# Dense matmuls inside the block inverses, a reordered load in the third quarter, and eight temporaries in a hybrid RWKV-7 and sparse-attention layer

## The chip, the cores and the metric

The kernel runs on one core of one Trainium2 chip. The metric is the device time of one execution in microseconds (us). Times of the kernel before are a median of three runs. A separate execution is recorded by the hardware profiler; its own time is given beside them. Engines are named as in the profile: PE is TensorE, DVE is VectorE, ACT is ScalarE, POOL is GpSimd, SP is the engine that only issues DMAs. A small q after an engine's name stands for its instruction sequencer, where DMA issues are shown.

## The reference

One decoder layer over 1024 tokens of width 1024, in float32. A normalised input is multiplied by one wide matrix. Its columns feed two branches that are computed side by side and merged by sigmoid gates:

```python
proj = rmsnorm(h, norm1_g) @ w_in            # -> p_rwkv, p_att, p_idx, p_gate
y_a = rwkv7_mix(token_shift(p_rwkv, tshift_mu), ...)
y_b = dsa_attention(rope(q), rope(k), v, rope(q_idx), rope(k_idx), w_idx)
g_a, g_b = split(sigmoid(p_gate))
h = h + (g_a * (y_a @ w_o_rwkv) + g_b * (y_b @ w_o_att)) @ w_out
h = h + (silu(z_gate) * z_up) @ w_ffn_out    # z = rmsnorm(h) @ w_ffn_in
return rmsnorm(h, normf_g)
```

The RWKV branch is a recurrence over tokens with a 64 x 64 state for each of 8 heads:

```python
sa = einsum('bhij,bhj->bhi', state, -kk_t)
state = state * d_t + sa[..., None] * (kk_t * a_t) + v_t[..., None] * k_t
y_t = einsum('bhij,bhj->bhi', state, r_t)
```

The attention branch lets each query see the 256 keys with the highest index scores.

## The kernel before, in words

**Two kinds of matmul.** The wide products (projections, gates, output matrices, feed-forward) are split into high and low parts so that three matmuls of 128 x 128 by 128 x 512 make one product of near-float32 accuracy. `mm3` (lines 137 to 149) issues them and is a generator: it yields after every few matmuls how many it has issued. This text calls them dense matmuls. The RWKV branch works on small tiles with long chains between PE, ACT and DVE.

**Filling.** Generators of dense work wait in a queue named `fill`. `pump(n)` (lines 177 to 186) adds n to a credit and runs the first generator until the credit is used up; a generator that yields more than is left makes the credit negative, which the next call pays off. So dense matmuls stand between the small ones, at places and in numbers that are written into the code. `ticks(n, m)` (lines 190 to 194) pumps n in m portions and after each portion advances a second generator, `beside[0]`, by one step: a bisection for the attention's selection (`select`, lines 979 to 1054), which runs on ACT and DVE. The order of instructions on PE is the order of the program text (manual_schedule, line 1700). The order on ACT, DVE, POOL and SP is fixed when the program is built, by a list scheduler that follows program order as far as it believes operands and buffers to be ready. At run time each engine and each DMA queue works through its list in order.

**Temporaries.** `tmp()` (lines 112 and 113) gives a 128 x 512 float32 tile from the pool `tp`, which has 4 such slots (line 58). A slot is free again when the last reader of the tile is done, and that can be a DMA that stores it. Tiles from `tmp()` hold gate values on their way to DRAM (lines 515 to 518), parts of the selection (lines 1029 to 1032), the attention's result on its way to DRAM (lines 1171, 1190 and 1191) and the gates that the merge loads (lines 1281 to 1284).

**The RWKV quarters.** `rwkv` (lines 548 to 909) handles 512 tokens per call, in two quarters of 256. Quarter q has two pairs of 64-token chunks, `pr` 0 and 1. In each quarter:

- Lines 701 to 722: masked products `MT` are made, and their 32 x 32 diagonal blocks are stored to DRAM (`d_n`, line 721).
- Lines 740 to 753: the blocks are loaded with other axes (`N`, line 742) and DVE inverts them by a recursion of 31 steps in `W`.
- Lines 754 to 767: the inverses go through DRAM (`d_w`, lines 755 and 764) into `TT`; DVE transposes a part of them into `TZ` (line 767).
- Lines 769 to 774: a row of sums is loaded, broadcast over 64 partitions (`P`, line 771), and POOL multiplies it (line 774).
- Line 775: `ticks` covers this chain with dense matmuls.
- Lines 778 to 785: for each `pr`, 32 x 32 matmuls (line 781) from `TZ` into PSUM, and ACT copies them back to `TZ` (line 784).
- Lines 787 to 798: `inner(0)`, a product for the right-hand side (line 791), then `pump(4)`.
- Lines 799 to 806: for each `pr`, the second 32 x 32 matmuls (line 802), which read that copy; ACT copies the result to `TT` (line 805).
- Lines 832 to 909: the recurrence over four chunks with three matmul groups each (lines 843, 862 and 874), with pumps between.

While quarters 0 and 1 run, `fill` holds projections, gates and the attention of the first 512 tokens (`att0`). From quarter 2 on it holds `merge(0)` and the feed-forward part of the first 512 tokens (`ffn`). `merge` (lines 1274 to 1340) loads two gate tiles per output column block d in `gates(d)` (lines 1280 to 1284), those of d = 0 ahead of the rest. All of the loads and stores named here are issued by SP, except the gate stores of line 518, which ACT issues, as it does the weight loads of line 123 in this part of the kernel.

Of the kernel before, what the change touches and what calls it, by code (L numbers as in the profile page):

```python
# [51 lines left out]
def block_kernel(ctx: ExitStack, tc: tile.TileContext, ins: dict, outT: bass.AP, outR: bass.AP, stop=None, dbg=None):  # L52
    nc = tc.nc
    V, A, G, T, SY = nc.vector, nc.scalar, nc.gpsimd, nc.tensor, nc.sync

    cp = ctx.enter_context(tc.tile_pool(name="cp", bufs=1))
    wp = ctx.enter_context(tc.tile_pool(name="wp", bufs=2))
    tp = ctx.enter_context(tc.tile_pool(name="tp", bufs=4))
    dp = ctx.enter_context(tc.tile_pool(name="dp", bufs=1, space=bass.MemoryType.DRAM))
    psA = ctx.enter_context(tc.tile_pool(name="psA", bufs=3, space=bass.MemoryType.PSUM))  # L60
    psM = ctx.enter_context(tc.tile_pool(name="psM", bufs=5, space=bass.MemoryType.PSUM))
# [24 lines left out]
    def scratch(name, shape):  # L86
        return [dp.tile(shape, F32, name=f"{name}{h}") for h in range(2)]
# [8 lines left out]
    d_g = scratch("d_g", [16, 128, HT])  # L96
# [4 lines left out]
    d_bs = [dp.tile([2, 4, 256], F32, name=f"d_bs{q}") for q in range(4)]  # L101
    d_n = [dp.tile([64, 32, 32], F32, name=f"d_n{q}") for q in range(4)]
# [74 lines left out]
    def pump(n):  # L177

        credit[0] += n
        while credit[0] > 0 and fill:  # L180
            try:
                credit[0] -= abs(next(fill[0]))
            except StopIteration:
                fill.popleft()
        if not fill:
            credit[0] = 0
# [3 lines left out]
    def ticks(n, m):  # L190

        for i in range(m):
            pump(n * (i + 1) // m - n * i // m)
            next(beside[0], None)
# [331 lines left out]
    def rwkv_consts(p):  # L526
# [18 lines left out]
        p.tile([128, 64], F32, name="edge")  # L545
        return cmask, wup, gup, rmask, ind, ind16

    def rwkv(half, p, consts, ready=None, settled=None):
        cmask, wup, gup, rmask, ind, ind16 = consts

        def t4(tag, shape=(128, 4, 256)):
            return p.tile(list(shape), F32, tag=tag, name=tag)

        for q in range(2 * half, 2 * half + 2):
# [184 lines left out]

            N = p.tile([128, 32, 32], F32, tag="x6", name="N")  # L740
            for par_ in range(2):
                SY.dma_start(N[64 * par_:64 * par_ + 64], d_n[q])
            W = p.tile([128, 16, 32], F32, tag="x7", name="W")
            V.memset(W, 0.0)
            for par_ in range(2):
# [22 lines left out]

            bsp = t4("P")
            for e in range(2):  # L770
                SY.dma_start(bsp[64 * e:64 * e + 64].rearrange("p c t -> p (c t)"),
                             d_bs[q][e].rearrange("c s -> (c s)").partition_broadcast(64))
            bon = v
            G.tensor_tensor(bon, v, bsp, op=ALU.mult)
            ticks((209, 231, 281, 232)[q], (13, 4, 10, 6)[q])
            both = [(h, pa, 64 - 64 * pa, 64 * pa) for h in range(8) for pa in range(2)]
            hd = [(h, h // 2, slice((h % 2) * 64, (h % 2) * 64 + 64), slice(h * 64, h * 64 + 64)) for h in range(8)]
            for pr in range(2):
                ps = mix()
                for h, pa, ba, kb in both:  # L780
                    T.matmul(ps[ba + 32:ba + 64, h * 32:(h + 1) * 32], MT[2 * pr + pa][ba:ba + 32, h, ba + 32:ba + 64],
                             TZ[ba:ba + 32, 0, pr, h, :], start=True, stop=True)
                for ba in (64, 0):
                    A.activation(TZ[ba + 32:ba + 64, 1, pr, :, :],
                                 ps[ba + 32:ba + 64, 0:256].rearrange("p (h t) -> p h t", h=8), AF.Copy)

            def inner(pr):
                ps = mix()
# [44 lines left out]
            for pr in range(2):  # L833
                yb = p.tile([128, 2, 512], F32, tag=("P", "x6")[pr], name="yb")
                yc, y2 = yb[:, 0, :], yb[:, 1, :]
                for pa in range(2):
                    c = 2 * pr + pa
# [436 lines left out]
    def merge(half, zp, zs):  # L1274
        yt = yhi, ylo = act_tiles(zp, "y", ("s0", "s1"))
        mt = act_tiles(zp, "m", ("s2", "s3"))
        for j in range(8):
            SY.dma_start(ylo[:, j, :].bitcast(F32), (d_ya if j < 4 else d_yb)[half][j % 4])

        def gates(d):  # L1280
            ga, gb = tmp(), tmp()
            SY.dma_start(ga, d_g[half][d])
            SY.dma_start(gb, d_g[half][8 + d])
            return ga, gb

        first_gates = gates(0) if half == 0 else None
        yield 0
        for j in range(8):
            split(yhi[:, j, :], ylo[:, j, :], ylo[:, j, :].bitcast(F32))
        yield -30  # L1290
        ahead = [weights(ins["w_o"][d]) for d in range(2)] if half == 0 else []
        for d in range(8):
            w = ahead[d] if d < len(ahead) else weights(ins["w_o"][d])
            ga, gb = first_gates if half == d == 0 else gates(d)
            pa = acc()
            pb = None
            if half == d == 0:
                pb = acc()
                yield from mm3_two((pa, pb), w, yt)
            else:  # L1300
                yield from mm3(pa, w, yt, nk=4)
            with tc.high_priority() if pb else nullcontext():
                V.scalar_tensor_tensor(ga, ga, 1.0, pa, op0=ALU.add, op1=ALU.mult)
                if pb:
                    V.scalar_tensor_tensor(gb, gb, 1.0, pb, op0=ALU.add, op1=ALU.mult)
            if pb is None:
                pb = acc()
                yield from mm3(pb, w, yt, nk=4, wk=4, ak=4)
                V.scalar_tensor_tensor(gb, gb, 1.0, pb, op0=ALU.add, op1=ALU.mult)
            V.tensor_tensor(ga, ga, gb, op=ALU.add)  # L1310
            A.activation(mt[0][:, d, :], ga, AF.Copy, scale=0.5)
            V.scalar_tensor_tensor(mt[1][:, d, :], ga, 0.5, mt[0][:, d, :].bitcast(F32), op0=ALU.mult,
                                   op1=ALU.subtract)
        yield -10
        h = zp.tile([128, 8, HT], F32, tag="s0", name="h")
        load_x(half, h, range(8))
        sq = Rms(h)
        zt = zhi, zlo = act_tiles(zp, "z", ("s1", "s3")) if half == 0 else (None, None)
        pss = []
        if half == 0:  # L1320
            pss = [acc(), acc()]
            yield from mm3_last(pss, [weights(ins["w_out"][d]) for d in range(2)], mt, 8)
        for d in range(8):
            if d < len(pss):
                ps = pss[d]
            else:
                ps = acc()
                yield from mm3(ps, weights(ins["w_out"][d]), mt)
            V.tensor_tensor(h[:, d, :], h[:, d, :], ps, op=ALU.add)
            if half == 0:  # L1330
                A.activation(zhi[:, d, :], h[:, d, :], AF.Copy, scale=par[:, P_N2 + d:P_N2 + d + 1])
            SY.dma_start(d_h[half][d], h[:, d, :])
            sq.add(d)
        if half == 1:
            zs.append(sq)
            return
        for d in range(8):
            V.scalar_tensor_tensor(zlo[:, d, :], h[:, d, :], par[:, P_N2 + d:P_N2 + d + 1],
                                   zhi[:, d, :].bitcast(F32), op0=ALU.mult, op1=ALU.subtract)
        zs.extend((zt, sq))  # L1340
# [548 lines left out]
```

## Time and profile before

| what | value |
|---|---|
| median of 3 runs | 1706.21 us (1706.05 to 1706.52) |
| profiled execution, its own time | 1709.14 us |
| its span, first to last instruction | 1707.2 us |
| mean granted clock of TensorE | 0.996 |
| first 32 x 32 matmuls (line 781) of quarters 0, 1, 2, 3 | 426.5, 575.5, 739.4, 895.0 us |
| busy time of PE, DVE, ACT, POOL | 1686.1, 1180.9, 896.4, 97.3 us |

How to read it: the page has six sections: busy time by engine, a picture of the span in 40 slices, DMA queues, the chain of work that ended last, the costliest groups of instructions, and DMA issues. Other views of the same trace list who waited for whom, the instructions in order of time, and the busy time in chosen stretches. In the view in order of time each row has the start, the length, the engine, the line, the operation, the tiles (written <- read), the shapes, how many were merged, and in brackets the idle time before it with what ended it. Matmuls overlap: a matmul's own length is longer than the distance to the next one's start.

### The profile page before, as it was taken

The page shows a single profiled execution, that of the slowest core. Times are in us where ns is not written, and L with a number is a line of the kernel's source. Part 1 is how long each engine was busy: PE and PEld are TensorE (multiplying, and loading weights), DVE is VectorE, ACT ScalarE, POOL GpSimd, SP SyncE. Part 2 cuts the span into 40 slices and gives each one's busy share as a digit, 9 for nine tenths or more (in the row PEclk, how much of TensorE's full clock was granted, in tenths as well). Part 3 has the DMA queues.
Part 4 walks back from the last instruction along what each step waited for, and adds up shares of the span by engine and source line. Part 5 has one row for each costly group of instructions (what it writes and reads, how often), then busy time and mean ns, then how long its engine had stood idle before and what let it go on. Part 6 is the DMA issues. An engine that isn't in the chain of part 4 may idle for free.

```text
span 1707.2 us, 28295 instructions
## 1 busy us (share of the span) xinstructions
PE 1686.1 (99%) x10802; PEld 1419.4 (83%) x10802; DVE 1180.9 (69%) x2305; ACT 896.4 (53%) x1727; POOL 97.3 (6%) x107
## 2 busy tenths in 40 slices
PE   9999999999999999999999999999999999999998
PEld 8888888878878777878787888878888899899998
DVE  6789889967567458957886655535564885675764
ACT  6365998453554588755334365533323544353452
POOL 0000000000021110000200110000000000000002
PEclk9999999999999899999999999999999999999999
DMA  6542334436257525653343633244455344524532
GB/s 220 178 136 91 98 104 149 147 108 181 98 177 213 153 95 170 207 171 109 106 123 97 213 128 120 76 154 166 145 185 187 113 156 131 183 95 144 169 113 99
DMA packets 142231, 243.58 MB, mean 143 GB/s; under 512 B 48864, under 2 KB 71072, under 8 KB 141968
## 3 DMA queue, kind: packets, MB, share of 16 engines
q1 hardware_dynamic: 119360, 170.76, 31.3%
q10 hardware_dynamic: 16128, 48.60, 8.5%
q0 software_dynamic: 6608, 22.42, 4.2%
q8 instruction: 85, 1.39, 0.3%
q14 instruction: 50, 0.41, 0.1%
HBM read 188.73 MB, written 53.00 MB: 142 GB/s over the span
## 4 chain that ended last, share of the span: by engine, by line
PE 87%; DVE 5%; DMA 3%; ACT 2%; issue 1%; POOL 1%; SPq 0%; ACTq 0%; POOLq 0%; DVEq 0%
PE acc L142 18%; PE acc L147 18%; PE acc L143 18%; PE acc L160 3%; PE mix L1597 3%; PE mix L1595 3%; PE mix L1594 3%; PE mix L1154 2%; PE mix L958 2%; PE mix L1144 2%; PE mix L1128 1%; PE acc L417 1%; DVE wlo L117 1%; PE mix L142 1%; PE acc L1597 1%
## 5 line engine op out<-in xcount | busy, mean ns | idle before, releaser
L117 DVE TENSOR_TENSOR wlo<-wst,whi 128x1024 fp32r<-128x1024 f32 (+1 forms) x203 | 246.4, 1216 | 181.2 <-PE acc L147 73.9
L116 ACT ACTIVATE whi<-wst 128x1024 fp32r<-128x1024 f32 (+1 forms) x203 | 212.3, 1048 | 185.7 <-PE acc L143 137.1
L142 PE MATMUL acc<-zhi,whi 128*128 128x512 f32 x400 | 158.8, 397 | 0.0
L143 PE MATMUL acc<-zlo,whi 128*128 128x512 f32 x400 | 156.1, 390 | 0.0
L142 PE MATMUL acc<-u1hi,whi 128*128 128x512 f32 x320 | 128.5, 401 | 0.0
L143 PE MATMUL acc<-u1lo,whi 128*128 128x512 f32 x320 | 125.5, 392 | 0.0
L142 PE MATMUL acc<-u0hi,whi 128*128 128x512 f32 (+1 forms) x320 | 122.8, 386 | 0.0
L143 PE MATMUL acc<-u0lo,whi 128*128 128x512 f32 (+1 forms) x320 | 121.3, 382 | 0.0
L147 PE MATMUL acc<-zhi,wlo 128*128 128x512 f32 x400 | 103.1, 395 | 0.0
L142 PE MATMUL acc<-fhi,whi 128*128 128x512 f32 x234 | 91.9, 393 | 0.6 <-ACT whi L116 0.5
L143 PE MATMUL acc<-flo,whi 128*128 128x512 f32 x234 | 91.1, 390 | 0.0
L142 PEld LDWEIGHTS acc<-zhi,whi 128*128 128x128 f32 x400 | 75.1, 188 | 16.9 <-issue 1.8
L143 PEld LDWEIGHTS acc<-zlo,whi 128*128 128x128 f32 x400 | 75.2, 188 | 14.7
L147 PEld LDWEIGHTS acc<-zhi,wlo 128*128 128x128 f32 x400 | 73.6, 188 | 15.6 <-issue 1.2
L147 PE MATMUL acc<-u1hi,wlo 128*128 128x512 f32 x320 | 82.5, 398 | 0.0
L147 PE MATMUL acc<-u0hi,wlo 128*128 128x512 f32 (+1 forms) x320 | 78.7, 384 | 0.0
L1008 ACT ACTIVATE junkl<-kept,z 128x1024 int8<-128x1024 int16 (+1 forms) x64 | 69.4, 1084 | 4.6 <-DVE kept L977 4.4
L142 PEld LDWEIGHTS acc<-u1hi,whi 128*128 128x128 f32 x320 | 60.3, 189 | 12.7 <-issue 0.9
L147 PEld LDWEIGHTS acc<-u1hi,wlo 128*128 128x128 f32 x320 | 59.6, 190 | 12.8 <-issue 0.9
L142 PEld LDWEIGHTS acc<-u0hi,whi 128*128 128x128 f32 x320 | 60.2, 188 | 11.9 <-issue 0.4
L143 PEld LDWEIGHTS acc<-u1lo,whi 128*128 128x128 f32 x320 | 60.5, 189 | 11.3
L143 PEld LDWEIGHTS acc<-u0lo,whi 128*128 128x128 f32 x320 | 60.2, 188 | 11.0
(455 smaller groups left out, 4041.0 us busy)
## 6 DMA issues: line engine op xcount, KB each, us to landing
wst<-in_w_ffn_in SPq DMA_DIRECT2D x72, 512.0 KB, 3.8
wst<-in_w_in ACTq DMA_DIRECT2D x36, 512.0 KB, 3.9
wst<-in_w_in SPq DMA_DIRECT2D x25, 512.0 KB, 4.3
wst<-in_w_fo SPq DMA_DIRECT2D x25, 512.0 KB, 3.5
h<-in_xT SPq DMA_DIRECT2D x32, 256.0 KB, 5.2
d_g<-tmp ACTq DMA_DIRECT2D x32, 256.0 KB, 2.8
k<-d_k POOLq DMA_DIRECT2D x16, 512.0 KB, 5.8
tmp<-d_g SPq DMA_DIRECT2D x32, 256.0 KB, 3.0
```

The costliest lines, as they stand in the source:

```text
L116: A.activation(hi, x, AF.Copy)
L117: V.tensor_tensor(lo, x, hi.bitcast(F32), op=ALU.subtract)
L142: T.matmul(ps, whi[:, wk + k, :], ahi[:, ak + k, tok], start=k == 0, stop=False)
L143: T.matmul(ps, whi[:, wk + k, :], alo[:, ak + k, tok], start=False, stop=False)
L147: T.matmul(ps, wlo[:, wk + k, :], ahi[:, ak + k, tok], start=False, stop=k == nk - 1)
L160: T.matmul(ps, w[:, k, :], a[:, k, tok], start=k == 0 and j == 0, stop=k == nk - 1 and j == 2)
L958: T.matmul(ps[:, :w], iq[:, h, :], ik[:, i, c:c + w], start=i == 0, stop=i == 1)
L1008: A.activation(junka[:, :n], y, AF.Sign, bias=z[:, i:i + 1], accum_out=cnt[:, i:i + 1])
L1144: T.transpose(ps[:, j * 128:(j + 1) * 128], L[:, (c + j) * 128:(c + j + 1) * 128], ident)
L1594: T.matmul(ps, whi[:, k, :], ahi[:, k, :], start=opens and k == 0, stop=False, skip_group_check=True)
L1595: T.matmul(ps, whi[:, k, :], alo[:, k, :], start=False, stop=False, skip_group_check=True)
L1597: T.matmul(ps, wlo[:, k, :], ahi[:, k, :], start=False, stop=k == 3, skip_group_check=True)
```

## The change

It has three parts.

1. In every quarter, `pump(4)` follows each of the two bursts of line 781 and its ACT copies. The `ticks` ahead of them pump 202, 223, 281 and 226 where they pumped 209, 231, 281 and 232.
2. In quarter 2, the two loads of line 771 are issued after the loads of the mask blocks (`N`, line 742), and in `merge(0)` the gate loads of d = 1 to 7 are issued after them too.
3. The pool `tp` gets 8 slots in place of 4, and the scratch for the descriptors of POOL's DMAs is set to 8192 bytes a partition, where its size had been left at the builder's own.

```diff
-    tp = ctx.enter_context(tc.tile_pool(name="tp", bufs=4))
+    tp = ctx.enter_context(tc.tile_pool(name="tp", bufs=8))
...
+    third = []
+
     def rwkv(half, p, consts, ready=None, settled=None):
...
             for par_ in range(2):
-                SY.dma_start(N[64 * par_:64 * par_ + 64], d_n[q])
+                asked = SY.dma_start(N[64 * par_:64 * par_ + 64], d_n[q])
+            if q == 2:
+                third.append(asked)
...
             for e in range(2):
-                SY.dma_start(bsp[64 * e:64 * e + 64].rearrange("p c t -> p (c t)"),
-                             d_bs[q][e].rearrange("c s -> (c s)").partition_broadcast(64))
+                with tc.issue_after(asked.ins) if q == 2 else nullcontext():
+                    SY.dma_start(bsp[64 * e:64 * e + 64].rearrange("p c t -> p (c t)"),
+                                 d_bs[q][e].rearrange("c s -> (c s)").partition_broadcast(64))
...
-            ticks((209, 231, 281, 232)[q], (13, 4, 10, 6)[q])
+            ticks((202, 223, 281, 226)[q], (13, 4, 10, 6)[q])
...
                     A.activation(TZ[ba + 32:ba + 64, 1, pr, :, :],
                                  ps[ba + 32:ba + 64, 0:256].rearrange("p (h t) -> p h t", h=8), AF.Copy)
+                pump(4)
...
             ga, gb = tmp(), tmp()
-            SY.dma_start(ga, d_g[half][d])
-            SY.dma_start(gb, d_g[half][8 + d])
+            with tc.issue_after(third[0].ins) if half == 0 and d else nullcontext():
+                SY.dma_start(ga, d_g[half][d])
+                SY.dma_start(gb, d_g[half][8 + d])
...
-    nc = bacc.Bacc("TRN2", target_bir_lowering=False, num_devices=1)
+    nc = bacc.Bacc("TRN2", target_bir_lowering=False, num_devices=1, dynamic_dma_scratch_size=8192)
```

`tc.issue_after(x)` adds no wait between engines; it fixes that what its block issues on x's engine stands behind x in that engine's order.

## The prediction

> **What bounds the kernel now.** I read the page first (busy times, clock), then who waited for whom on PE, then instructions in order of time around the inverses of the four quarters.
>
> ```profile
> PE 1686.1 (99%) x10802; PEld 1419.4 (83%) x10802; DVE 1180.9 (69%) x2305; ACT 896.4 (53%) x1727; POOL 97.3 (6%) x107
> ...
> PEclk9999999999999899999999999999999999999999
> ```
>
> PE is busy from end to end, no other engine but its own weight loads (PEld) above 69%. So only three things move the time: PE standing still, PE running at a lower clock, or PE paying for a change between kinds of matmul. Slice 14 of the clock row, from 555 to 598 us, is the one that is not full. The second quarter's inverse lies in it.
>
> ```profile
> PE mix L802 <- ACT TZ L784: 2.7, 3, 2.3
> PE mix L710 <- DVE MT L714: 1.9, 2, 1.1
> ...
> PE mix L781 <- DVE TZ L767: 0.7, 1, 0.7
> ```
>
> Columns: total us, times, longest. The longest wait of PE, 2.3 us, stands before line 802, behind the ACT copy of line 784. The changed lines can reach the first and third rows.
>
> **The second quarter: the wait and the clock.** PE in order of time there, then PE's clock by 5 us (PEclk is the column ahead of the DMA share).
>
> ```profile
> 578.48 0.40 PE L143 MATMUL acc<-u1lo,whi 128*128 128x512 f32 x1
> 581.21 2.31 PE L802 MATMUL mix<-TT,TZ 32*32 32x32 f32 x64 [2.33 <-ACT TZ L784]
> 583.45 1.97 PE L843 MATMUL mix<-S,AR 64*128 64x64 f32 x16
> ```
>
> ```profile
> 575.00:580.00 5.00, 3.88 (x104) 3.07 (x102) 1.38 (x4) 1.94 (x5) 0.00 (x0) 1.00 0.99 361
> 580.00:585.00 5.00, 3.71 (x79) 3.51 (x80) 1.44 (x3) 4.82 (x12) 0.00 (x0) 0.56 0.07 21
> 585.00:590.00 5.00, 5.00 (x29) 3.92 (x30) 1.59 (x6) 3.65 (x11) 1.20 (x2) 0.50 0.07 17
> 590.00:595.00 5.00, 5.00 (x46) 3.49 (x44) 2.49 (x4) 3.05 (x9) 0.76 (x1) 0.91 0.26 61
> ```
>
> For the ordinary handover I use the first quarter, where nothing waits:
>
> ```profile
> 422.79 1.98 PE L147 MATMUL acc<-u0hi,wlo 128*128 128x512 f32 x8
> 424.60 0.39 PE L142 MATMUL acc<-u0hi,whi 128*128 128x512 f32 x1
> ...
> 426.50 1.20 PE L781 MATMUL mix<-TZ,MT 32*32 32x32 f32 x64
> 427.63 1.15 PE L791 MATMUL mix<-UV,MT 64*64 64x64 f32 x32
> 428.71 0.50 PE L142 MATMUL acc<-u0hi,whi 128*128 128x512 f32 x1
> ...
> 429.51 0.39 PE L143 MATMUL acc<-u0lo,whi 128*128 128x512 f32 x1
> 429.83 1.20 PE L802 MATMUL mix<-TT,TZ 32*32 32x32 f32 x64
> ```
>
> There 429.51 to 429.83 is 0.32 us; in the second quarter 578.48 to 581.21 is 2.73. The wait costs 2.41 us. After it the clock is at half: shares of 0.56, 0.50 and 0.91 missing 0.44, 0.50 and 0.09 of 5 us each are 5.15 us of lost clock, that is 10.3 us at half speed. It begins in the second stretch, 4.4 us of which are at half, so near 580.6, 0.6 us before PE restarts. The part under work is 9.7 us, and costs 4.85 us. The same is seen directly: a burst of 64 small matmuls takes 2.24 us (581.21 to 583.45) against 1.13 (426.50 to 427.63).
>
> Why was the copy late?
>
> ```profile
> 574.54 0.71 ACT L1030 ACTIVATE tmp<-kept,top 128x512 f32<-128x512 int16 x1
> ...
> 576.46 0.18 ACT L1114 ACTIVATION_READ_ACCUMULATOR L<-L,mx 128x1 f32 x1
> 578.91 1.84 ACT L1030 ACTIVATE tmp<-kept,top 128x512 f32<-128x512 int16 x3 [2.26 <-DMA d_yb<-tmp]
> 580.78 1.57 ACT L784 ACTIVATE TZ<-mix 32x256 f32<-32x256 f32 x4
> ```
>
> ```profile
> 567.08 0.46 SPq L1191 DMA_DIRECT2D d_yb<-tmp  x1
> ```
>
> ACT's list has four copies of line 1030, each into a fresh temporary, ahead of line 784. The second waits 2.26 us for a DMA that stores a temporary, issued at 567.08 and so nearly 12 us under way while the DMA share is 0.99. Four slots are not enough for stores that land this late. With eight, the slot comes from a tile four allocations older: this wait goes, and 2.41 + 4.85 = 7.26 us of PE with it.
>
> What is late next there: ACT is free at 576.64, three copies take 1.84, then line 784 takes 1.57 and ends at 580.05; its first half, which the first burst of line 802 needs, at 579.27. PE would reach line 802 at 578.48 + 0.32 = 578.80, less 8 ticks, plus the two new groups of dense matmuls (below: 8 x 0.226 = 1.81 off, 2 x 1.12 on), so at 579.23. I leave 0.2 us of wait, between 0 and 1.2.
>
> **The third quarter.**
>
> ```profile
> 739.44 0.75 PE L781 MATMUL mix<-TZ,MT 32*32 32x32 f32 x34
> 740.92 0.69 PE L781 MATMUL mix<-TZ,MT 32*32 32x32 f32 x30 [0.73 <-DVE TZ L767]
> 741.53 1.15 PE L791 MATMUL mix<-UV,MT 64*64 64x64 f32 x32
> ...
> 743.43 0.40 PE L143 MATMUL acc<-mlo,whi 128*128 128x512 f32 x1
> 744.06 0.24 PE L802 MATMUL mix<-TT,TZ 32*32 32x32 f32 x2 [0.24 <-ACT TZ L784]
> ...
> 745.88 1.11 PE L843 MATMUL mix<-S,AR 64*128 64x64 f32 x16
> ```
>
> Line 781 takes 2.09 us to the next line here against 1.13: 0.96 lost. The gap before line 802 is 0.63 against 0.32, and line 802 itself 1.82 against 1.13: 0.31 + 0.69. Together 1.96 us. The new dense group between the halves of line 781 delays the second by 1.12, more than its wait of 0.73. Line 802 comes 2.24 later, more than its 1.00. I count the 1.96 as gone, with 1.0 as the lower bound.
>
> The moved loads add little by themselves:
>
> ```profile
> 674.48 4.61 SPq L721 DMA_DIRECT2D d_n<-MT  x8
> 679.14 1.13 SPq L771 DMA_DIRECT2D P<-d_bs  x2
> 680.77 1.08 SPq L742 DMA_DIRECT2D N<-d_n  x2
> 681.91 0.58 SPq L1282 DMA_DIRECT2D tmp<-d_g  x1
> ```
>
> The load of the blocks reads what line 721 has just stored, and between the end of line 771's issues (680.27) and line 742 (680.77) SP stood still. So going first wins less than the 1.63 us of the issue times, and perhaps nothing; what stands behind, line 771 and the gates of d = 1, moves back by about as much. POOL's product from line 771 is first read in `finish`, after a whole pair. The gates already stood behind line 742 here; the new order keeps that when eight slots would have let them ahead. I count 0, between 1 lost and 1 won.
>
> **What the new dense groups cost.** A dense matmul in a row takes (424.60 - 422.79) / 8 = 0.226 us, so four are 0.91. Between small bursts, the four from 428.71 to the next burst at 429.83 take 1.12: 0.21 more, since entering and leaving the small tiles costs time. The group that cuts line 781 in two also pays for one more end of a burst.
>
> ```profile
> L781 PE MATMUL mix<-TZ,MT 32*32 32x32 f32 x256 | 5.0, 192 | 0.7 <-DVE TZ L767 0.7
> ```
>
> A burst of 1.20 less one matmul of 0.19 has its last start at 1.01, the next line starts at 1.13: 0.12 for an end. So 0.33 for the first group and 0.21 for the second, 0.54 a quarter, 2.16 in four. The lower bound is 1.5: in the fourth quarter the dense generator goes in steps of seven (line 165, nk of 8), so a credit of 4 is not spent in a group each time. The upper is 2.8, if pieces of attention, in small matmuls themselves, fall into the groups of the second quarter. The three waits of line 802 and the one of line 781 in the list of waits are all shown above, so in quarters 0 and 3 nothing waits at these lines and the groups are cost alone.
>
> The dense matmuls themselves are moved, not added: ticks and groups sum to +1, 0, +8 and +2 over the quarters. The shorter ticks bring line 781 forward by 7, 8 and 6 x 0.226 = 1.59, 1.81 and 1.36 us. It would then be due at 424.91 in quarter 0, at 573.66 in quarter 1 and at 893.68 in quarter 3, and the last `TZ` is ready before that in each:
>
> ```profile
> 423.09 0.42 DVE L767 STREAM_TRANSPOSE TZ<-TT 32x256 f32<-32x256 f32 x1
> ...
> 566.64 1.35 DVE L767 STREAM_TRANSPOSE TZ<-TT 32x256 f32<-32x256 f32 x3
> ...
> 890.46 0.42 DVE L767 STREAM_TRANSPOSE TZ<-TT 32x256 f32<-32x256 f32 x1
> ```
>
> The least cover is 1.4 us, in quarter 0 (423.51 to 424.91). Were it gone, PE would wait by what is missing.
>
> **Eight slots and the small scratch elsewhere.** The scheduler places ACT, DVE and SP work anew all over the kernel. No row shows what comes of that; the nearest is PE's longest other wait, the 1.1 us of line 710. I take 0, between 2.5 lost and 2 won.
>
> **The sum.** Against the profiled execution's own 1709.14 us: - 2.41 - 4.85 + 0.2 - 1.96 + 2.16 = - 6.86, so 1702.28. The median of the runs is 2.93 lower than that execution (1706.21), and I take the same off: 1699.35, rounded to 1699.3. By the bounds above this case lies between 1696 and 1702.7. The measurement of this kernel can tell about 0.2% from no change, 3.4 us: faster is below 1702.8, slower above 1709.6.
>
> [...] In this trace PE idle for 2.33 us was followed by half the clock, while the other waits in the list above, up to 1.1 us, left no mark in the clock row. [...]
>
> **Rivals.**
>
> First, the drop of the clock belongs to the profiled execution and not to the timed runs. Then 4.85 us of the gain are not there to be had: 1704.15, no measurable change. For it: the profiled execution is 2.93 us longer than the median. Against it: the three runs lie within 0.47 us, so they all had the drop or none did, and the idle time comes from the order of instructions, the same in each. [...] Chance 0.11.
>
> Second, the wait changes hands. ACT still comes late to line 784, held by DVE or by a DMA while the DMA share is near 1, PE stands still for about 2 us and the clock falls again. The 7.26 us stay, 1.96 go and 2.16 come: 1706.4. For it: ACT's list keeps four copies of line 1030 ahead, and its cover is thin (579.27 against 579.23). Against it: to reach 2 us something must be late by that much, and only the slot was. Chance 0.12.
>
> Third, on the other side: eight slots let the dense stream's evacuations run ahead, and the scheduler puts one of them in front of a link of the recurrence.
>
> ```profile
> 424.85 1.22 DVE L117 TENSOR_TENSOR wlo<-wst,whi 128x1024 fp32r<-128x1024 f32 x1 [1.34 <-ACT whi L116]
> ```
>
> `pump(8)` covers a link with 8 x 0.226 = 1.8 us. One such operation of 1.22 in front fits, two do not. It decides once PE stands still for 2.3 us in one place: then that costs 7.26. Two places, with the gain as forecast: 1699.3 + 14.5 = 1713.8. For it: the new order is unknown, and 12 chunks outside the second quarter have no reserve of ACT or DVE beyond the pumps. Against it: those links pass here with waits below 1 us. Chance 0.09.
>
> Fourth, the halved scratch holds POOL back. It issues few, large pieces, 6608 packets of 22.42 MB in all:
>
> ```profile
> q0 software_dynamic: 6608, 22.42, 4.2%
> ```
>
> I give it 0.01; its loads are issued two blocks ahead of use.
>
> **How the numbers follow.** The forecast with its variants holds 0.67, all of it faster. The first two rivals, 0.23, are no measurable change; the third and fourth, 0.10, slower. Range: 1696.0 to 1706.4 takes in the forecast's bounds, the first rival and the near half of the second; outside remain the slower cases and the far ends, near 0.2.
>
> **What would show it.** Right: PE's clock row full in slice 14; no wait of PE for line 784 above 0.5 us; line 1030 on ACT in a row without a DMA in its bracket; line 781 in eight halves with dense matmuls behind each, about 1.1 us from a group's start to the next burst; DVE's line 767 no longer before PE in the third quarter. Wrong: a PE wait of about 2 us anywhere with a clock below 9 in its slice; the second quarter's bracket still there; or a full clock in slice 14 and yet less than 3 us gained in the timed runs, which is the first rival.

## The result, and the profile after

The changed kernel takes 1728.03 us (median of four runs, 1726.33 to 1730.61) against 1706.37 for the kernel before on the same chip: a ratio of 1.012, 95% interval 1.0104 to 1.0136. It is slower by about 21 us. The forecast was 1699.3.

The profiled execution took 1730.61 us, its span is 1728.2 against 1707.2. Line numbers of the changed kernel are those of its own text: 781 became 786, 784 789, 802 808, 1030 1036, 742 744, 771 776, 751 and 753 755 and 757, 1303 1310, 655 657, 710 712. The page of after has these lines for the busy time and for PE's clock by slices:

```profile
PE 1694.3 (98%) x10802; PEld 1422.7 (82%) x10802; DVE 1186.1 (69%) x2305; ACT 899.3 (52%) x1727; POOL 95.5 (6%) x107
...
PEclk9999999999999999999999999999999999999999
```

PE stands still for 1728.2 - 1694.3 = 33.9 us; before it was 1707.2 - 1686.1 = 21.1. So 12.8 us of the loss are PE waiting. Slice 14 of the clock row has become a 9, and so has every other: the row looks better than before. It can't show what happened, since a slice is 43 us long. PE's clock in six short stretches of after:

```profile
509.00:513.00 4.00, 4.00 (x17) 3.52 (x18) 3.59 (x5) 3.35 (x5) 0.87 (x2) 0.57 1.04 281
584.00:588.00 4.00, 4.00 (x35) 3.35 (x28) 1.15 (x4) 2.10 (x5) 0.00 (x0) 0.57 0.02 5
697.00:701.00 4.00, 3.63 (x9) 2.88 (x10) 3.14 (x9) 0.55 (x3) 0.00 (x0) 0.57 0.74 273
802.00:807.00 5.00, 5.00 (x22) 4.33 (x22) 1.73 (x8) 1.99 (x6) 1.01 (x1) 0.66 0.09 26
850.00:855.00 5.00, 4.36 (x32) 3.95 (x30) 3.82 (x7) 1.01 (x2) 0.00 (x0) 0.66 0.45 102
1372.00:1377.00 5.00, 4.23 (x12) 3.34 (x13) 3.83 (x6) 3.69 (x4) 0.00 (x0) 0.66 0.00 0
```

PEclk is the column ahead of the DMA share. A share of 0.57 of 4 us lacks 1.72, one of 0.66 of 5 us lacks 1.70. Inside them the share is 0.50 (511 to 512 and 585 to 586 us), so it is 3.4 us at half speed each time. Six of them cost 3 x 1.72 + 3 x 1.70 = 10.3 us, where before had one drop of 5.15, 4.85 of it while PE worked. So the lower clock adds 5.4 us. Waiting and clock together are 18.2 of the 21.0 us by which the span grew; the remaining 2.8 is of the size of the handovers forecast for the new groups (2.16).

Who waited for whom on PE in after (total us, times, longest):

```profile
PE acc L142 <- DVE tmp L1310: 5.4, 1, 5.4
PE mix L712 <- DVE MT L716: 2.7, 3, 1.4
PE mix L880 <- ACT UV L871: 2.3, 3, 0.9
PE mix L657 <- ACT nrT L651: 1.4, 1, 1.4
...
PE mix L808 <- issue: 1.3, 1, 1.3
PE acc L1356 <- ACT yhi L116: 1.2, 1, 1.2
```

Part of this stood before too: line 710 (712 here) with 1.9 us in two waits, line 874 (880 here) with 0.7 in one. Only one of these rows, line 808, lies in the chain that the new groups were put into. The rest is elsewhere: between 507 and 1373 us, from the second quarter's normalisation (657) to the feed-forward part. The places that the prediction worked on did improve. The second quarter in after, PE in order of time:

```profile
581.48 1.00 PE L808 MATMUL mix<-TT,TZ 32*32 32x32 f32 x51
583.79 0.38 PE L808 MATMUL mix<-TT,TZ 32*32 32x32 f32 x13 [1.31 <-issue]
```

ACT at the same place:

```profile
577.10 0.71 ACT L1036 ACTIVATE tmp<-kept,top 128x512 f32<-128x512 int16 x1
...
577.72 1.83 ACT L1036 ACTIVATE tmp<-kept,top 128x512 f32<-128x512 int16 x3
579.57 1.58 ACT L789 ACTIVATE TZ<-mix 32x256 f32<-32x256 f32 x4
```

The four copies run in a row, no DMA in a bracket, and line 808 starts without waiting for line 789. Then its burst stands still for 1.31 us behind its 51st matmul, with no engine and no load named as the reason (the section on the prediction comes back to it), and the clock halves from 584.5. Of the forecast's 2.41 + 4.85 us, 1.31 + 1.72 are there again: 4.2 less than in the profile before, not 7.06. And the third quarter:

```profile
747.02 0.69 PE L786 MATMUL mix<-TZ,MT 32*32 32x32 f32 x32
747.64 0.50 PE L142 MATMUL acc<-mhi,whi 128*128 128x512 f32 x1
...
748.77 0.69 PE L786 MATMUL mix<-TZ,MT 32*32 32x32 f32 x32
...
752.74 1.20 PE L808 MATMUL mix<-TT,TZ 32*32 32x32 f32 x64
```

No row has a bracket, so the 1.96 us of waits there are gone. Against the one profile of before, some 6.2 us were won at the places that the prediction looked at (4.2 and 1.96); other executions, under part 3, show that both amounts vary without any change. As the span grew by 21.0, some 27 were lost, of which the prediction had seen 2.16 coming.

### The profile page after: what moved, and what is told of

Its sections match the earlier page's. It is cut to its first block, busy times and chain, and to the rows that moved or that the text cites. A ratio compares the mean times of both kernels' runs of the same rounds, so it can differ in the third digit from the quotient of the medians.

```text
span 1728.2 us, 28265 instructions
## 1 busy us (share of the span) xinstructions
PE 1694.3 (98%) x10802; PEld 1422.7 (82%) x10802; DVE 1186.1 (69%) x2305; ACT 899.3 (52%) x1727; POOL 95.5 (6%) x107
## 3 DMA queue, kind: packets, MB, share of 16 engines
q8 instruction: 85, 1.39, 0.3%
## 4 chain that ended last, share of the span: by engine, by line
PE 87%; DVE 7%; ACT 2%; DMA 1%; issue 1%; POOL 1%; SPq 0%; POOLq 0%; DVEq 0%; ACTq 0%
PE acc L142 19%; PE acc L143 18%; PE acc L147 18%; PE acc L160 3%; PE mix L1604 2%; PE mix L1602 2%; PE mix L1601 2%; PE mix L1160 2%; PE mix L964 2%; PE mix L1150 2%; DVE wlo L117 1%; PE mix L1134 1%; PE acc L417 1%; PE mix L142 1%; PE acc L1604 1%
```

## The experiments

The theory after the result was that one of the three parts makes PE wait far from where it was put, through the order in which the scheduler places ACT, DVE and SP. The rivals were the other parts, and the handovers of the groups. All ratios are to the kernel before on the same chip, with 95% intervals; several chips were used. 0.1% is 1.7 us. Every kernel computes the whole layer. Each diff shows the lines that matter, with `...` where others stand between or are left out.

### The three parts alone

**a_slots**, part 3 alone:

```diff
+    tp = ctx.enter_context(tc.tile_pool(name="tp", bufs=8))
...
+    nc = bacc.Bacc("TRN2", target_bir_lowering=False, num_devices=1, dynamic_dma_scratch_size=8192)
```

> Eight slots and the 8 KB scratch alone, ticks and load order as before. Theory (order): the second quarter's wait of 2.4 us and its half clock go, as forecast (-7.3), and the selection's last steps, which now stand earlier on DVE in the fourth quarter, cost 2 to 6 us of PE waits there: 1700 to 1706 us. Rival (slots are the whole loss): 1720 us or more, with PE waits spread over all quarters. Rival (dense groups are the whole loss): 1699 us.

Measured: 1710.38 us, 1.0014 (0.9998 to 1.003). The second quarter's slot wait was gone:

```profile
580.64 1.24 PE L802 MATMUL mix<-TT,TZ 32*32 32x32 f32 x48 [0.15 <-ACT TZ L784]
582.07 0.41 PE L802 MATMUL mix<-TT,TZ 32*32 32x32 f32 x14 [0.19 <-issue]
```

No wait above 0.2 us is left there, and the kernel isn't faster: slower than the theory's 1700 to 1706 and far from the rival's 1720.

**b_dense**, part 1 alone:

```diff
-            ticks((209, 231, 281, 232)[q], (13, 4, 10, 6)[q])
+            ticks((202, 223, 281, 226)[q], (13, 4, 10, 6)[q])
...
+                pump(4)
```

> The dense groups and shorter ticks alone, four slots, old load order. Theory (order): the second quarter's wait on a slot stays, the groups cost about 2 us in handovers, and shorter ticks move other instructions so that some new waits of 1 to 1.5 us appear: 1706 to 1716 us. Rival (dense groups are the whole loss): 1724 us or more, with no single wait above 1 us but longer handovers at every group. Rival (slots are the whole loss): 1705 us.

Measured: 1723.13 us, 1.0101 (1.008 to 1.0122). That is most of the loss. It lies between the theory's range, up to 1716, and the rival's 1724.

**c_order**, part 2 alone:

```diff
+                with tc.issue_after(asked.ins) if q == 2 else nullcontext():
+                    SY.dma_start(bsp[64 * e:64 * e + 64].rearrange("p c t -> p (c t)"),
...
+            with tc.issue_after(third[0].ins) if half == 0 and d else nullcontext():
```

> The load order of the third quarter alone. Theory (order): the wait of 5.4 us before the second column block of the merge comes with this part, followed by half the clock: 1711 to 1716 us. Rival (the wait comes from slots or dense groups): no such wait, 1705 to 1707 us.

Measured: 1713.05 us, 1.0038 (1.0023 to 1.0053). It has one new long wait, also there in after. PE in c_order:

```profile
693.38 0.50 PE L142 MATMUL acc<-yhi,whi 128*128 128x512 f32 x1 [3.94 <-DVE tmp L1309]
```

### The pairs, and the table of all eight

**bc**: parts 1 and 2.

```diff
+            ticks((202, 223, 281, 226)[q], (13, 4, 10, 6)[q])
...
+                pump(4)
...
+            with tc.issue_after(third[0].ins) if half == 0 and d else nullcontext():
```

> Dense groups and load order, with four slots and the old scratch: the changed kernel without its third part. Theory (order): at least as slow as the changed kernel, since the second quarter's wait on a slot is not removed: 1720 to 1735 us. Rival (slots are the whole loss): 1705 to 1708 us.

Measured: 1730.74 us, 1.0139 (1.011 to 1.0167).

**ac**: parts 2 and 3.

```diff
+    tp = ctx.enter_context(tc.tile_pool(name="tp", bufs=8))
...
+            with tc.issue_after(third[0].ins) if half == 0 and d else nullcontext():
```

> Eight slots, scratch and load order, without dense groups and with the old ticks. Theory (order): the second quarter's wait is gone, the wait before the merge's second column block is there: 1706 to 1716 us. Rival (dense groups are the whole loss): 1699 us. Rival (slots are the whole loss): 1720 us or more.

Measured: 1714.34 us, 1.0033 (1.0017 to 1.0048).

**ab**: parts 1 and 3.

```diff
+    tp = ctx.enter_context(tc.tile_pool(name="tp", bufs=8))
...
+            ticks((202, 223, 281, 226)[q], (13, 4, 10, 6)[q])
...
+                pump(4)
```

> Eight slots, scratch and dense groups, with the old load order. Theory (order): the changed kernel less the wait of 5.4 us and its half clock of 3.5 us: 1717 to 1722 us. Rival (the load order does nothing): 1726 to 1731 us as the changed kernel.

Measured: 1722.15 us, 1.007 (1.0046 to 1.0094).

| per cent over before | without part 1 | with part 1 |
|---|---|---|
| neither 2 nor 3 | 0 | 1.01 |
| part 3 (slots) | 0.14 | 0.70 |
| part 2 (loads) | 0.38 | 1.39 |
| parts 2 and 3 | 0.33 | 1.20 |

Read along the rows, part 1 costs 1.01, 0.56, 1.01 and 0.87, on average 0.86%. Part 2 costs 0.38, 0.19, 0.38 and 0.50, on average 0.36%. Part 3 gives +0.14, -0.31, -0.05 and -0.19, on average -0.10% with an uncertainty of about 0.13, and none of the four is outside its own. The sum of the three averages, 1.12%, agrees with the 1.20% (1.04 to 1.36) of the whole change.

### Part 1: the groups or the shift

The ticks and groups of part 1 add up to +1, 0, +8 and +2 matmuls over the four quarters. The rivals were that the groups themselves cost more than forecast, and that the shift does.

**b_phase**, the shift without any group:

```diff
-            ticks((209, 231, 281, 232)[q], (13, 4, 10, 6)[q])
+            ticks((210, 231, 289, 234)[q], (13, 4, 10, 6)[q])
```

> No dense group inside the inverses, and ticks of 210, 231, 289 and 234: the dense stream stands, behind each inverse, where it stands with the groups and shorter ticks, which is +1, 0, +8 and +2 matmuls from where it stood before. Theory (the shift of the dense stream against the small chains is the loss): as slow as the dense part alone, 1718 to 1724 us, with its waits before the lines of the key normalisation in quarter 1, the merge, the mask products of quarter 3 and the recurrence of quarter 3. Rival (the groups and their handovers are the loss): 1706 us.

Measured: 1726.65 us, 1.0119 (1.0097 to 1.0141). Three of the four numbers in one line changed, and nearly the whole loss is there, a little more than the theory's 1718 to 1724. PE's waits in b_phase:

```profile
PE mix L655 <- ACT nrT L649: 2.8, 2, 1.4
PE mix L802 <- ACT TZ L784: 2.8, 2, 2.6
PE mix L710 <- DVE MT L714: 2.4, 3, 1.4
PE acc L1349 <- ACT yhi L116: 2.3, 1, 2.3
PE mix L874 <- ACT UV L865: 2.0, 3, 0.9
```

Four of these are the lines of after (657, 712, 1356, 880 there), without a single group. The wait of line 802 is the one of the kernel before.

**b_zero**, the groups without the shift:

```diff
-            ticks((209, 231, 281, 232)[q], (13, 4, 10, 6)[q])
+            ticks((201, 223, 273, 224)[q], (13, 4, 10, 6)[q])
...
+                pump(4)
```

> The dense groups inside the inverses, with ticks of 201, 223, 273 and 224, so that each quarter pumps as many matmuls up to the end of the inverse as before. Theory (shift): the waits elsewhere are gone and the groups' handovers of about 2 us are left, 1706 to 1711 us. Rival (groups and handovers): 1720 us or more.

Measured: 1714.17 us, 1.0032 (1.0017 to 1.0047). This is above the theory's 1711 and below the rival's 1720. The order still isn't that of before, and there is a new wait of 1.3 us at line 631, and one of 1.1 at line 781 where before had 0.7.

**a_b_zero**, b_zero with part 3:

```diff
+    tp = ctx.enter_context(tc.tile_pool(name="tp", bufs=8))
...
+            ticks((201, 223, 273, 224)[q], (13, 4, 10, 6)[q])
...
+                pump(4)
```

> Eight slots and the 8 KB scratch with the dense groups and ticks of 201, 223, 273 and 224, old load order: the version that theory (shift) picks. If the groups cover the copies of the inverse and the slots end the second quarter's wait, 1702 to 1708 us; if the slots' new order costs as much as alone, 1708 to 1712. Rival (groups): 1720 us or more.

Measured: 1709.09 us, 1.001 (0.9997 to 1.0023). So the groups cost +0.32% on before, -0.04% on a_slots (0.10 against 0.14) and -0.18% on b_phase (1.01 against 1.19): 0.03% on average, and the forecast's 2.16 us (0.13%) lies within what these differences can tell. The shift costs 1.19% on before, 0.69% on b_zero and 0.60% on a_b_zero.

Which quarter's shift? The rivals were a sum over the quarters, and the third quarter's shift by eight alone.

**b_q0**, **b_q2** and **b_q3**, one quarter each:

```diff
+            ticks((210, 231, 281, 232)[q], (13, 4, 10, 6)[q])
```

In b_q2 the same line is:

```diff
+            ticks((209, 231, 289, 232)[q], (13, 4, 10, 6)[q])
```

And in b_q3:

```diff
+            ticks((209, 231, 281, 234)[q], (13, 4, 10, 6)[q])
```

> Only the first quarter's dense stream is shifted, by one matmul (ticks 210, 231, 281, 232), no groups. Theory A, each quarter's shift brings the waits of the places whose lists it changes, and the costs add up to the 1.2% of all three shifts together: the lists of PE, DVE and ACT change in 227, 176 and 186 rows here, in the first half of the kernel, so 0.2 to 0.5%, with the waits near 508 and 601 to 615 us and none of those after 900 us. Theory B, the place is what counts and nearly all of the loss comes from the third quarter's shift by eight, which rewrites the lists of the whole second half: no more than 0.15% here.

> Only the third quarter's dense stream is shifted, by eight matmuls (ticks 209, 231, 289, 232), no groups. Theory A, the costs of the three shifts add up: 0.5 to 0.8% here, with the waits near 842 to 851 and 923 to 940 us but not those near 508 and 601 to 615. Theory B, nearly all of the loss comes from this one: 0.9 to 1.2%.

> Only the fourth quarter's dense stream is shifted, by two matmuls (ticks 209, 231, 281, 234), no groups. Theory A, the costs of the three shifts add up: 0.1 to 0.4%, with waits of about 1 us near 923 to 940 or 1363 to 1373 us. Theory B, nearly all of the loss comes from the third quarter's shift: no more than 0.15%.

Measured, in this order: 1720.87 us, 1.0076 (1.0057 to 1.0095); 1714.25 us, 1.0037 (1.0022 to 1.0052); 1711.16 us, 1.0023 (1.001 to 1.0036). They add up to 1.36%, with an uncertainty of 0.27, against 1.19% for all three. So the sum agrees with costs that add, and theory B falls. The cost does not go by the size of the shift: one matmul in the first quarter costs most, 13 us, more than the 0.5% that theory A had as its upper end, and eight in the third cost less than its 0.5 to 0.8%.

One of its waits can be followed to the cause. ACT in the kernel before, in order of time:

```profile
504.22 1.04 ACT L116 ACTIVATE whi<-wst 128x1024 fp32r<-128x1024 f32 x1
...
505.16 0.36 ACT L649 ACTIVATE nrT<-mix 16x256 fp32r<-16x256 f32 x1
...
507.87 0.63 ACT L517 ACTIVATE tmp<-tmp 128x512 f32<-128x512 f32 x1 [2.35 <-DVE tmp L516]
```

The same place on ACT in b_q0:

```profile
508.33 0.63 ACT L517 ACTIVATE tmp<-tmp 128x512 f32<-128x512 f32 x1 [2.61 <-DVE tmp L516]
508.87 0.36 ACT L649 ACTIVATE nrT<-mix 16x256 fp32r<-16x256 f32 x1
```

And on PE in b_q0:

```profile
509.28 0.74 PE L655 MATMUL mix<-nrT,ind 16*128 16x256 f32 x4 [1.42 <-ACT nrT L649]
```

Before, line 517, the evacuation of the next output block, stands behind line 649 in ACT's list; in b_q0 it stands ahead of it. That the scheduler does so because it believes the block to be ready earlier is inferred from the two lists. At run time line 517 waits 2.61 us for DVE, line 649 comes after it, and PE, which needs line 649's result now, stands still for 1.42 us. PE's own order moves too, and by more than one matmul, since the dense generator goes in pieces: between lines 647 and 655 stand 12 dense matmuls before and 8 in b_q0. After has the same wait, before 508.84. The waits of the other two are again at their own places. Who waited on PE in b_q2:

```profile
PE mix L710 <- DVE MT L714: 2.7, 3, 1.4
PE mix L255 <- DVE sacc L249: 1.7, 2, 1.3
```

The same view of b_q3:

```profile
PE acc L143 <- DVE zlo L117: 1.2, 1, 1.2
```

They are those of after at 847 to 851 and 800 us, and at 1371 to 1373 us. The wait of line 710 in b_q2 has the same kind of cause. DVE there:

```profile
839.34 1.28 DVE L714 TENSOR_TENSOR MT<-mix,cmask 128x512 f32<-128x512 f32 x2
840.53 0.68 DVE L1390 SCALAR_TENSOR_TENSOR tmp<-tmp 128x512 f32<-128x512 f32 x1
```

The evacuation of line 1390 now stands between the steps of line 714; before, it ran at 833.10 and seven steps of line 714 ran in a row. The long reach of a shift shows in the order of the traces too: against before, 817 rows of PE, 215 of DVE and 183 of ACT in b_phase don't fall into the common order, and 69, 53 and 97 in b_zero.

### Part 2: which of the loads

**c_sum**, only line 771 behind line 742, the gates free:

```diff
+                with tc.issue_after(asked.ins) if q == 2 else nullcontext():
+                    SY.dma_start(bsp[64 * e:64 * e + 64].rearrange("p c t -> p (c t)"),
...
```

> Only the two loads of the row of sums stand behind the mask blocks in the third quarter; the gate loads keep their place. Theory (the list scheduler, seeing the mask blocks come earlier, puts more steps of the recursion ahead of the evacuation of the merge's second column block): the wait of about 4 us is there, 1713 us as with the whole load order. Rival (the later gate loads cause it): 1706 us.

Measured: 1707.39 us, 1.0 (0.9987 to 1.0013), and the wait isn't there: that expectation was wrong. The gates' constraint alone leaves the compiled order of every engine as it was, so there was nothing to measure. It takes both. SP in after, in order of time:

```profile
681.83 1.13 SPq L744 DMA_DIRECT2D N<-d_n  x2
683.00 1.24 SPq L776 DMA_DIRECT2D P<-d_bs  x2
684.27 0.59 SPq L1289 DMA_DIRECT2D tmp<-d_g  x1
```

The gates of d = 1 start at 684.27 where they started at 681.91, and DVE's list has the recursion ahead of the step that needs them. DVE in after:

```profile
689.50 3.14 DVE L117 TENSOR_TENSOR wlo<-wst,whi 128x1024 fp32r<-128x1024 f32 x1 [1.63 <-ACT whi L116]
692.56 0.18 DVE L755 TENSOR_TENSOR tw<-W,N 128x31 f32<-128x31 f32 x1
...
696.63 0.68 DVE L1310 SCALAR_TENSOR_TENSOR tmp<-tmp,acc 128x512 f32<-128x512 f32 x1
```

The same place on DVE before:

```profile
690.24 0.18 DVE L751 TENSOR_TENSOR tw<-W,N 128x31 f32<-128x31 f32 x1
690.46 0.19 DVE L753 TENSOR_TENSOR W<-W,tw 128x31 f32<-128x31 f32 x1
690.57 0.68 DVE L1303 SCALAR_TENSOR_TENSOR tmp<-tmp,acc 128x512 f32<-128x512 f32 x1
```

One pair of recursion steps stood ahead of the evacuation before, eight pairs do now, 4 us in all. PE waits for the PSUM tile that this evacuation empties. The scheduler's belief about the later gates is inferred from the two lists; that the two constraints together make the wait is shown by c_order beside c_sum.

### Part 3: the slots, and how much of the drop was there

**own3**, the forecast's mechanism by itself: three slots of their own for the tiles of line 1030, with the small scratch.

```diff
-                t = tmp()
+                t = tp.tile([128, HT], F32, tag="sel", name="sel", bufs=3)
```

> The kernel before, where only the selection's copies of line 1030 get three slots of their own, and the scratch is 8 KB to make room. It tests the forecast's mechanism by itself: with the slot there, the second quarter's wait of 2.3 us and the half clock behind it go. Theory: 1699 us, if the new order of ACT and DVE brings no other wait; up to 1706 if it does. Rival (the wait is not the slot's): the wait of about 2 us before the second burst stays, 1706 us.

Measured: 1719.95 us, 1.0061 (1.0039 to 1.0083). Theory and rival both fail: the slot wait is gone and the kernel is slower, by waits in the first quarter's normalisation (3.02 us before 368.24) and in a projection (3.32 us before 398.63):

```profile
PE mix L647 <- DVE nr L117: 3.8, 3, 3.0
PE mix L478 <- ACT tmp L493: 3.3, 1, 3.3
```

Where line 1030 runs, with first and last start, in own3:

```profile
L1030 ACT ACTIVATE sel<-kept,top x4: 601/708/708, 297.4 to 301.3; 128x512 f32<-128x512 int16 x3, 128x384 f32<-128x384 int16 x1
```

And before:

```profile
L1030 ACT ACTIVATE tmp<-kept,top x4: 602/707/722, 574.5 to 580.1; 128x512 f32<-128x512 int16 x3, 128x384 f32<-128x384 int16 x1
```

The shortage of slots had held the selection back. With slots of its own the scheduler places these steps nearly 280 us earlier, and the bisection behind them (line 1008 on ACT) ends at 421 us and not at 728, so all of it shares ACT and DVE with the first quarter's links. From 340 to 420 us PE is idle for about 11 us in own3 and for 0.3 before.

**s_scratch**, only the scratch. The order of instructions is that of before on every engine, so it also serves as a second look at the kernel before.

```diff
+    nc = bacc.Bacc("TRN2", target_bir_lowering=False, num_devices=1, dynamic_dma_scratch_size=8192)
```

> The 8 KB descriptor scratch alone. The instructions and their order are the same as before. Theory: 1706 us, no change. Rival (POOL held back by the small scratch): 1708 us or more, with POOL's loads landing later than 5.8 us.

Measured: 1707.55 us, 0.9989 (0.9975 to 1.0003). The scratch costs nothing. The second quarter in this execution, ACT first:

```profile
579.89 1.84 ACT L1030 ACTIVATE tmp<-kept,top 128x512 f32<-128x512 int16 x3 [0.58 <-DMA d_yb<-tmp]
```

PE in the same execution:

```profile
582.18 0.24 PE L802 MATMUL mix<-TT,TZ 32*32 32x32 f32 x2 [0.65 <-DMA d_g<-tmp]
```

With the same order, the wait for the slot is 0.58 us here where it was 2.26, PE's wait 0.65 where it was 2.33, and no half clock follows. The DMA that stores the tile lands earlier or later from one execution to the next. On one chip 25 runs of the kernel before lie between 1704.19 and 1712.64 us.

The eleven traces with four shared slots (before, s_scratch, c_sum, c_order, b_dense, bc, b_phase, b_zero and the three single quarters) show how far this goes. Line 1030 waits for a DMA in all eleven, between 0.58 and 2.55 us. PE's wait before line 802 is between 0 and 2.62 us, on average 1.3, and PE loses between 0 and 5.1 us of clock from 576 to 602 us, on average 2.6. In the five traces with eight slots no such wait is left, and clock is lost only in after. So the forecast's mechanism is there, worth some 3.9 us on average and not 7.26, since the one profile of before was near the upper end.

The third quarter varies too. PE in s_scratch, with the order of before:

```profile
738.08 1.20 PE L781 MATMUL mix<-TZ,MT 32*32 32x32 f32 x64
```

The waits in the third quarter that the forecast took for 1.96 us aren't there, without any group.

## Why the prediction was wrong

The step that failed is "The dense matmuls themselves are moved, not added: ticks and groups sum to +1, 0, +8 and +2 over the quarters". The sums were right, and their cost was counted at nothing. Shifting the dense stream by those sums costs 1.19% by itself (20 us), and 0.60 to 0.69% where the groups stand already. PE's order is hand-written, but the lists of ACT and DVE are placed by the scheduler and change with the shift: 183 and 215 of their rows in b_phase don't fall into the common order with before. That the change goes by where a dense block ends against the small chains is the author's estimate. Two of the waits were followed to such a change of order; for the others it is inferred from their coming and going with the shift. The prediction said that the scheduler places work anew, yet tied it to the slots alone. None of its rivals reached the result: the slowest, the third, gave 1713.8.

**Load order, counted at 0, between 1 lost and 1 won:** 0.36% on average, 6 us. The cost of the issue on SP was the wrong thing to price; the list of DVE behind it was the right one.

**Eight slots, 2.41 + 4.85 us of gain:** the wait goes in every kernel that has them, as forecast, but the term was taken from an execution near the upper end. On average the place costs 3.9 us, and the time gained over the table is 0.10% (1.7 us), with an uncertainty of some 2 us. The argument that three runs within 0.47 us all had the drop was weak: s_scratch, with the same order, has none, and the runs of this kernel spread over 8 us. So the first rival, which took the drop for one execution's, was half right: nine of the eleven traces have a drop, most of them a smaller one. For **the slots elsewhere**, counted at 0, the nearest row was misread: PE's longest other wait before was the 1.2 us of line 396, not the 1.1 of line 710.

**What is late next, 0.2 us:** 1.31 us inside the burst of line 808, put down to "issue". It also stands in own3 (1.29), and is 0.22 or less in a_slots and s_scratch. The author's estimate is that PE's own instructions were loaded late. The page of after lists a DMA queue "q8 instruction" with 85 packets and 1.39 MB. One packet of it runs from 581.35 to 582.41, and PE goes on at 583.79, 1.38 us after its end. The 17 traces have ten such stops of PE above 0.15 us, and each of them ends 1.2 to 1.5 us after the end of a packet of this queue. Before, the packet was done at 580.10, while PE still waited for the slot (until 581.21), so the wait may have hidden it. No run changed the loading: this cause is argued from the times alone.

**Third quarter, 1.96:** the waits are gone in after, as forecast, but this says little. Line 781 has no wait there in six kernels without groups either (s_scratch, c_order, ac, b_q2, b_q3, b_phase), and in b_zero it waits 1.11 us although the groups are there. **Groups, 0.54 a quarter:** a group between two bursts takes 748.77 - 747.64 = 1.13 us in after where 1.12 was forecast, and the three differences that b_zero, a_b_zero and b_dense give average 0.03%.

**The third rival** had the kind of mechanism that decided, an evacuation put ahead of a link. It had it from the slots, at one or two places of 2.3 us or more. It came from the shift, at about a dozen places of 0.6 to 1.4 us; the loads added one of 5.4, where links were put ahead of an evacuation. A point of decision at 2.3 us left these out: the prediction took waits of up to 1.1 us for harmless, because they had left no mark in the clock row. In after, half clock began at 509.4 behind a wait of 1.42, at 584.5 behind 1.31 and at 803.0 behind 1.12. In b_q0 the same wait of 1.42 left the clock at full:

```profile
509.00:513.00 4.00, 3.72 (x22) 3.21 (x23) 3.22 (x6) 3.61 (x6) 1.29 (x2) 1.00 1.03 281
```

So a wait of little over 1 us may or may not cost clock, and it can be more than 1.7 us: in the second quarter waits of 1.15 (c_order) and 1.87 (b_q0) were followed by 3.4 us of lost clock, and 1.17 (b_q3) by none. The drop of before lasts 10.24 us, the six of after 3.41 each. Those six begin at 509.42, 584.51, 697.15, 802.97, 850.75 and 1372.99 us, and to 0.01 us the distances are 22, 33, 31, 14 and 153 times 3.4133. Behind the ends of the waits of 1.42, 1.31 and 1.12 they begin after 0.58, 0.72 and 2.12 us. Why a wait is followed by a drop in one execution and by none in another wasn't shown.

**What would show it:** the sign that slice 14 is full came true, and meant nothing: 3.4 us at half clock lower a slice of 43 us by 0.04 only. The sign named for the first rival, a full slice 14 without a gain, came true as well, though that rival foresaw no loss. The wait of 5.4 us did not set off the sign of being wrong, since that asked for a clock below 9 in its slice.

## What to carry to other kernels

Where one engine's order is written by hand and the others' are placed by a scheduler, a filler that is moved changes the whole kernel behind it: keep the sum per stretch the same to the matmul, and compare the compiled lists of every engine before pricing an edit. Even with equal sums b_zero cost 0.32%. Price an edit of load order or buffers by the lists that it rewrites, not by the wait that it removes. Before a wait is counted as a gain, look at it in a second execution of the same order.

None of the versions tried is faster than the kernel before: the nearest are s_scratch (0.9989, up to 1.0003), c_sum (1.0) and a_b_zero (1.001).

## What the runs showed of the hardware

PE's clock halved for 3.4 us, or for two or three times that (6.8 in b_q0 from 584.3, 10.2 before from 580.6). In after it did so behind waits of 1.12 to 1.42 us, above.

PE stopped for up to 1.31 us among small matmuls with no engine and no load to wait for. In all ten stops of this kind above 0.15 us it went on 1.2 to 1.5 us after the end of a packet of the instruction queue q8, above.

Line 117 on DVE lost nearly all of the time that it shared with POOL's operation. It takes 1.23 us alone; in after it took 3.14 (689.50, above) beside this one:

```profile
689.16 2.39 POOL L779 TENSOR_TENSOR v<-v,P 128x1024 f32<-128x1024 f32 x1 [31.58 <-DMA P<-d_bs]
```

They overlap from 689.50 to 691.55, 2.05 us, and line 117 is 1.91 longer. In b_dense, ab and before, overlaps of 1.91, 1.51 and 0.69 us made it 1.76, 1.37 and 0.53 longer. In bc line 117 started first, at 691.04: it took 1.23, and POOL's operation from 691.26 took 3.24 where it takes 2.39 to 2.58 in the others. Not every DVE instruction lost time: in c_sum lines 1304 and 1310, which read the PSUM tile `acc`, took 0.68 and 0.69 beside POOL's operation (687.53 to 690.01), against 0.69 for line 1304 alone, while line 1311 behind them, which reads `tmp` alone, took 1.47 where it takes 0.69. In after the overlap adds 1.9 us to DVE's path just ahead of the 5.37 us wait. It isn't shown to come from the later load of line 776: b_dense, ab and before have the overlap without that load order. In c_order and ac, which have that order, line 117 was clear of POOL's operation, and a step of the recursion took 2.28 and 2.42 us beside it, where such steps take 0.19 and 0.22.
